# A decoder trunk in fp32: the short convolution's transposes and the attention's value products issued differently

## Chip, cores and metric

One NeuronCore of a Trainium2 chip runs the whole program as one launch. The metric is device time in microseconds (us) of one execution, first to last instruction and what lies around them; the number given is the median of several executions.

## What is computed

Two layers over a sequence of 256 tokens with 1024 features: a half feed-forward block, a mixer, a second half feed-forward block and a gated embedding. The mixer is what the change touches. It projects its normed input to many pieces and runs three branches on them:

```
u = c_gate * xc
y = conv3(u)                       # causal, depthwise, 3 taps along the sequence
y_a = (b_gate * y) @ conv_w_out    # short convolution
y_m = mLSTM(...) @ mlstm_w_out
s = q·k (8 heads, 64 wide, one key and value head), masked to the 64 best keys
y_c = (softmax(s) @ v) @ attn_w_out
merged = g0*y_a + g1*y_m + g2*y_c  # then merged @ w_o
```

## The kernel before

All matrix products are made from fp32 numbers split in two: ScalarE writes the rounded half `wh` of a weight piece (`split`, L157), VectorE the rest `wl` (L158), and TensorE does three products per piece (`mm3`, L205 to L207). Weights come through five `raw` buffers: SyncE issues a transfer (L167) when VectorE has finished with the piece five before it. `project` goes through a projection in ticks of 12 products (4 pieces x 3), and after each tick calls `tick()`, which advances one generator in each of two queues. Those generators hold the side work of the mixer: `queues[0]` the sparse attention `dsa`, `queues[1]` gates and heads of the mLSTM, then `conv`, `conv_gate`, `mlstm_out`. What a generator emits gets a place among the products by a scheduler; every engine then works through its own list in that fixed order, so an instruction that waits holds up all behind it.

Tokens lie on partitions in two blocks `b` of 128; a transpose is needed wherever features must lie on partitions. There are two ways. `turn` (L279) does it on VectorE with 16 transposes of 32x32 pieces, L283. `pe_turn` (L289) does it on TensorE: four 128x128 transposes (L294) into a PSUM tile `tp`, then one copy by ScalarE (L295). There are two `tp` tiles and six PSUM tiles `acc`.

The parts that the change touches, all inside `mixer`:

- `conv` (L731): turns `ccn` to `uT` by `turn`, then 12 instructions of VectorE (L737, L740) make the three taps in `cv`.
- `conv_gate` (L751): turns `cbn` by `turn`, multiplies into `cv` (L755), splits the result (L157, L158).
- the end of `dsa` (L562 to L584): for a query block `b`, the softmax weights `ms` (maximum L551, L552; exponential L554 on ScalarE; L556 and L558 normalise, four heads at a time) are transposed, four heads of one parity `i` and one key block `sb` at a time (L570), copied by ScalarE to `pt` (L572), and multiplied with the values (`value`, L477). The heads of parity 0 write partitions 0 to 63 of their PSUM tile, those of parity 1 partitions 64 to 127. Query block 0 has one key block, query block 1 two. `todo` delays each product by one tick.

Of the kernel before, what the change touches and what calls it, by code (L numbers as in the profile page):

```python
# [13 lines left out]
ALU = mybir.AluOpType  # L14
AX = mybir.AxisListType

P = 128
T = 256
# [19 lines left out]
def trunk_kernel(  # L38
# [23 lines left out]
    def acc():  # L62
        return psum.tile([P, 512], F32, name=nm("acc"), tag="acc", bufs=6)
# [14 lines left out]
    def mid(shape, dt=F32):  # L78
        return spool.tile(list(shape), dt, name=nm("mid"), tag="mid", bufs=7)
# [199 lines left out]
    def turn(dst, src):  # L279

        for i in range(4):
            for j in range(4):
                nc.vector.transpose(  # L283
                    dst[32 * j:32 * j + 32].rearrange("p f (b i t) -> p b f i t", b=NB, i=4)[:, :, :, i, :],
                    src[32 * i:32 * i + 32].rearrange("p b (f j a) -> p b f j a", j=4, a=32)[:, :, :, j, :])
            if i < 3:
                yield
# [151 lines left out]
    def mixer(l, xs, next_norm):  # L439
# [36 lines left out]
        def value(ops, b, i, sb, pt):  # L476
            nc.tensor.matmul(ops[i][i * DH:(i + 1) * DH, :], avn[:, sb, :], pt.rearrange("p j t -> p (j t)"),  # L477
                             start=sb == 0, stop=sb == b)

        def dsa():  # L480
            akT = small([P, 2, T], "akT", 1)
            iqT = half([P, 2, T])
            aqT = mid([P, 4, T])
            for b in range(NB):
                tp = tps()
                for j in range(2):
                    nc.tensor.transpose(tp[:, j, :], kk[:, b, j].rearrange("p a d -> p (a d)"), ident)
                    nc.tensor.transpose(tp[:, 2 + j, :], iqn[:, b, j * P:(j + 1) * P], ident)
                nc.scalar.activation(akT[:, :, blk(b)], tp[:, 0:2, :], AF.Copy)
                nc.scalar.activation(iqT[:, :, blk(b)], tp[:, 2:4, :], AF.Copy)  # L490
                yield
            yield from turn(aqT, aqn)
            yield


            scores = []
            for b in range(NB):
                S = (b + 1) * P
                sc = small([P, S], f"score{b}", 1)
                for j in range(2):  # L500
                    ip = acc()
                    for h2 in range(2):
                        nc.tensor.matmul(ip[:, h2 * S:(h2 + 1) * S], iqT[j * DH:(j + 1) * DH, h2, blk(b)],
                                         akT[j * DH:(j + 1) * DH, 1, 0:S], start=True, stop=True)
                    rl = half([P, 2, S])
                    nc.scalar.activation(rl, ip[:, :2 * S].rearrange("p (a s) -> p a s", a=2), AF.Relu)
                    for h2 in range(2):
                        w = iw[:, b, 2 * h2 + j:2 * h2 + j + 1]
                        if h2 == 0 and j == 0:
                            nc.vector.tensor_scalar(sc, rl[:, h2, :], w, 0.0, op0=ALU.mult, op1=ALU.add)  # L510
                        else:
                            nc.vector.scalar_tensor_tensor(sc, rl[:, h2, :], w, sc, op0=ALU.mult, op1=ALU.add)
                dg = sc[:, b * P:(b + 1) * P]
                nc.gpsimd.affine_select(out=dg, in_=dg, pattern=[[-1, P]], compare_op=ALU.is_ge,
                                        fill=NEG, base=0, channel_multiplier=1)
                scores.append(sc)
                yield
            for b in range(NB):
                sc = scores[b]
                for i in range(N_SEL // 8):  # L520
                    m8 = small([P, 8], "m8")
                    nc.vector.max(out=m8, in_=sc)
                    nc.vector.match_replace(out=sc, in_to_replace=m8, in_values=sc, imm_value=GONE)
                    if i % 2 == 1:
                        yield
                nc.vector.tensor_scalar(sc, sc, -2e38, NEG, op0=ALU.is_ge, op1=ALU.mult)
                dg = sc[:, b * P:(b + 1) * P]
                nc.gpsimd.affine_select(out=dg, in_=dg, pattern=[[-1, P]], compare_op=ALU.is_ge,
                                        fill=NEG, base=0, channel_multiplier=1)
                yield  # L530


            for b in range(NB):
                S = (b + 1) * P
                bias = scores[b]
                ms = big([P, HA, S])
                for g in range(2):
                    for i in range(2):
                        sp = acc()
                        for q in range(2):  # L540
                            nc.tensor.matmul(sp[:, q * S:(q + 1) * S], aqT[i * DH:(i + 1) * DH, 2 * g + q, blk(b)],
                                             akT[i * DH:(i + 1) * DH, 0, 0:S], start=True, stop=True)
                        nc.vector.scalar_tensor_tensor(  # L543
                            ms[:, 4 * g + i:4 * g + 4:2, :], sp[:, :2 * S].rearrange("p (a s) -> p a s", a=2),
                            DH ** -0.5, bias[:, None, :].to_broadcast([P, 2, S]), op0=ALU.mult, op1=ALU.add)
                    yield
                mx = small([P, HA], "mx", 1)
                sm = small([P, HA], "sm", 1)
                for g in range(2):
                    hs = slice(4 * g, 4 * g + 4)  # L550
                    nc.vector.tensor_reduce(mx[:, hs], ms[:, hs, :], axis=AX.X, op=ALU.max)  # L551
                    nc.vector.tensor_scalar(mx[:, hs], mx[:, hs], -1.0, None, op0=ALU.mult)  # L552
                    for h in range(4 * g, 4 * g + 4):
                        nc.scalar.activation(ms[:, h, :], ms[:, h, :], AF.Exp, bias=mx[:, h:h + 1],  # L554
                                             accum_out=sm[:, h:h + 1])
                    nc.vector.reciprocal(sm[:, hs], sm[:, hs])  # L556
                    for h in range(4 * g, 4 * g + 4):
                        nc.vector.tensor_scalar(ms[:, h, :], ms[:, h, :], sm[:, h:h + 1], None, op0=ALU.mult)  # L558
                    yield
                yield  # L560

                ops = []  # L562
                todo = deque()
                for i in range(2):
                    op = acc()
                    ops.append(op)
                    for sb in range(b + 1):
                        tp = tps()
                        for j in range(4):
                            nc.tensor.transpose(tp[:, j, :], ms[:, 2 * j + i, blk(sb)], ident)  # L570
                        pt = half([P, 4, P])
                        nc.scalar.activation(pt, tp, AF.Copy)  # L572
                        todo.append((i, sb, pt))
                        yield
                        if len(todo) > 1:
                            value(ops, b, *todo.popleft())
                while todo:
                    value(ops, b, *todo.popleft())
                yield
                for i in range(2):  # L580
                    rows = slice(i * DH, (i + 1) * DH)
                    split(haT[rows, 0, :, blk(b)], haT[rows, 1, :, blk(b)],
                          ops[i][rows, :].rearrange("p (j t) -> p j t", j=4))
                yield  # L584
# [145 lines left out]

        def conv():  # L731
            uT = mid([P, 4, T])
            yield from turn(uT, ccn)
            yield
            for j in range(4):
                g = [gains[:, G_CONV + 12 * l + 4 * i + j:G_CONV + 12 * l + 4 * i + j + 1] for i in range(3)]
                nc.vector.tensor_scalar(cv[:, j, :], uT[:, j, :], g[2], None, op0=ALU.mult)  # L737
                for i in (1, 0):
                    s = 2 - i
                    nc.vector.scalar_tensor_tensor(cv[:, j, s:], uT[:, j, :T - s], g[i], cv[:, j, s:],  # L740
                                                   op0=ALU.mult, op1=ALU.add)
                yield
# [6 lines left out]
        ybT = big([P, 2, 4, T], F32R)  # L749

        def conv_gate():  # L751
            cbT = mid([P, 4, T])
            yield from turn(cbT, cbn)
            yield
            nc.vector.tensor_tensor(cv, cbT, cv, op=ALU.mult)  # L755
            split(ybT[:, 0], ybT[:, 1], cv)
            yield

# [237 lines left out]
```

## Time and profile before

| | |
|---|---|
| median of 3 runs | 1374.6 us (1374.56 to 1374.91) |
| the profiled execution | 1374.13 us, its span 1372.3 us |
| TensorE busy in the span | 1357.8 us (99%), 6156 products and transposes |
| VectorE busy | 1095.6 us (80%) |
| ScalarE busy | 722.6 us (53%) |
| mean granted TensorE clock | 0.998 of full speed |

Products overlap in TensorE, so its busy time is not the time that they need; the distance from one start to the next is. In the rows below, PE is TensorE, DVE VectorE, ACT ScalarE, SP SyncE; `L570` is line 570; `acc<-wh,xh` means that `acc` is written from `wh` and `xh`; `x4` counts merged instructions.

### The profile page before, as it was taken

To read this page: it belongs to the slowest core of one execution; us is meant where nothing else is said; L and a number is where in the kernel's file an instruction comes from. 1 tells how busy PE (TensorE), PEld (TensorE's weight loads), DVE (VectorE), ACT (ScalarE), POOL (GpSimd) and SP (SyncE) were. 2 spreads that over 40 slices of the span, in tenths; PEclk is the share of its full clock that TensorE was granted. 3 is DMA by queue.
4 is the path that set the end of the run, shared out by engine and by line. 5 is a ranking of instruction groups with operands and counts; after the bars stand their busy time and mean duration, and the time that the engine had idled before them with its cause. 6 is when DMAs were issued, how large, how long until landed. Compare 5 with 4: busy or idle time off the path is not lost.

```text
span 1372.3 us, 17274 instructions
## 1 busy us (share of the span) xinstructions
PE 1357.8 (99%) x6156; PEld 1110.4 (81%) x6156; DVE 1095.6 (80%) x2035; ACT 722.6 (53%) x1135; POOL 24.9 (2%) x42
## 2 busy tenths in 40 slices
PE   9999999999999999999999999999999999999997
PEld 7888888876788888888888888888768888888886
DVE  7988879879965687888788888797799566988876
ACT  6544466565544554444664444666565445444454
POOL 0000000000000000000000000000000000000000
PEclk9999999999999999999999999999999999999999
DMA  7855556533565556655556666565336645556661
GB/s 246 259 187 184 184 181 209 177 124 117 169 230 184 173 181 206 199 194 196 180 153 198 194 205 198 181 184 169 123 123 208 220 157 182 184 187 199 198 208 45
DMA packets 163427, 250.33 MB, mean 182 GB/s; under 512 B 7965, under 2 KB 101261, under 8 KB 163341
## 3 DMA queue, kind: packets, MB, share of 16 engines
q1 hardware_dynamic: 162700, 247.91, 56.6%
q0 software_dynamic: 352, 1.06, 0.2%
q8 instruction: 48, 0.79, 0.2%
q14 instruction: 39, 0.31, 0.1%
q10 hardware_dynamic: 288, 0.26, 0.1%
HBM read 248.14 MB, written 1.06 MB: 182 GB/s over the span
## 4 chain that ended last, share of the span: by engine, by line
PE 93%; DVE 5%; ACT 1%; issue 1%; POOL 0%; POOLq 0%; ACTq 0%
PE acc L205 24%; PE acc L207 24%; PE acc L206 24%; PE acc L402 18%; PE tp L264 2%; DVE mid L283 2%; DVE wl L158 1%; PE acc L693 1%; PE acc L477 1%; DVE mid L740 0%; DVE big L543 0%; DVE mx L551 0%; PE acc L128 0%; PE tp L570 0%; DVE big L558 0%
## 5 line engine op out<-in xcount | busy, mean ns | idle before, releaser
L158 DVE TENSOR_TENSOR wl<-raw,wh 128x1024 fp32r<-128x1024 f32 (+1 forms) x472 | 554.6, 1209 | 102.3 <-ACT wh L157 100.5
L157 ACT ACTIVATE wh<-raw 128x1024 fp32r<-128x1024 f32 (+1 forms) x472 | 473.7, 1043 | 201.3 <-issue 95.0
L205 PE MATMUL acc<-wh,xh 128*128 128x512 f32 (+1 forms) x1384 | 544.8, 394 | 0.8 <-ACT wh L157 0.8
L206 PE MATMUL acc<-wl,xh 128*128 128x512 f32 (+1 forms) x1384 | 538.3, 389 | 0.7 <-DVE wl L158 0.7
L207 PE MATMUL acc<-wh,xl 128*128 128x512 f32 (+1 forms) x1384 | 538.5, 389 | 0.0
L205 PEld LDWEIGHTS acc<-wh,xh 128*128 128x128 f32 x1384 | 260.6, 188 | 57.3 <-issue 3.9
L207 PEld LDWEIGHTS acc<-wh,xl 128*128 128x128 f32 x1384 | 260.3, 188 | 53.0
L206 PEld LDWEIGHTS acc<-wl,xh 128*128 128x128 f32 x1384 | 260.5, 188 | 52.0 <-DVE wl L158 1.2
L283 DVE STREAM_TRANSPOSE half<-half 32x128 f32<-32x128 f32 x640 | 193.9, 303 | 9.5
L402 PE MATMUL acc<-wh,mid 128*128 128x512 f32 x704 | 198.5, 392 | 0.0
L402 PEld LDWEIGHTS acc<-wh,mid 128*128 128x128 f32 x704 | 131.0, 188 | 27.3 <-ACT mid L267 0.9
L402 PE MATMUL acc<-wl,mid 128*128 128x512 f32 x352 | 108.6, 390 | 0.0
L157 ACT ACTIVATE mid<-half 128x512 fp32r<-128x512 f32 x40 | 25.3, 634 | 145.8 <-DVE half L283 145.8
L349 DVE SCALAR_TENSOR_TENSOR half<-acc,r,half 128x256 f32<-128x256 f32 x88 | 42.0, 480 | 74.6 <-ACT half L348 74.6
L348 ACT ACTIVATE half<-acc,r 128x256 f32<-128x256 f32 x88 | 41.5, 473 | 108.4 <-PE acc L207 108.4
L402 PEld LDWEIGHTS acc<-wl,mid 128*128 128x128 f32 x352 | 66.1, 188 | 13.8
L274 ACT ACTIVATE xh<-tp,gains 128x128 fp32r<-128x128 f32 x128 | 41.7, 363 | 19.8 <-PE tp L264 11.4
L206 PE MATMUL acc<-wl,big 128*128 128x512 f32 x128 | 50.0, 391 | 0.0
L207 PE MATMUL acc<-wh,big 128*128 128x512 f32 x128 | 49.9, 390 | 0.0
L205 PE MATMUL acc<-wh,big 128*128 128x512 f32 x128 | 49.8, 389 | 0.0
L275 DVE SCALAR_TENSOR_TENSOR xl<-tp,gains,xh 128x128 fp32r<-128x128 f32 x128 | 40.6, 346 | 8.5 <-ACT xh L274 7.7
L283 DVE STREAM_TRANSPOSE mid<-mid 32x256 f32<-32x256 f32 x96 | 41.8, 436 | 1.5
(184 smaller groups left out, 737.6 us busy)
## 6 DMA issues: line engine op xcount, KB each, us to landing
raw<-in_ffn_w_gu_dram SPq DMA_DIRECT2D x172, 512.0 KB, 5.3
raw<-in_w_in_dram SPq DMA_DIRECT2D x128, 512.0 KB, 4.1
raw<-in_ffn_w_down_dram SPq DMA_DIRECT2D x88, 512.0 KB, 4.7
raw<-in_mlstm_w_out_dram SPq DMA_DIRECT2D x16, 512.0 KB, 3.9
raw<-in_w_o_dram SPq DMA_DIRECT2D x16, 512.0 KB, 4.0
raw<-in_ple_w_gate_dram SPq DMA_DIRECT2D x16, 512.0 KB, 4.5
raw<-in_attn_w_out_dram SPq DMA_DIRECT2D x8, 512.0 KB, 3.7
raw<-in_conv_w_out_dram SPq DMA_DIRECT2D x8, 512.0 KB, 4.8
```

Of the source, the lines that this page charges most:

```text
L157: made = nc.scalar.activation(hi, v, AF.Copy).ins
L158: nc.vector.tensor_tensor(lo, v, hi.bitcast(F32), op=ALU.subtract)
L205: nc.tensor.matmul(ps, ah, wh, start=start, stop=False)
L206: nc.tensor.matmul(ps, ah, wl, start=False, stop=False)
L207: nc.tensor.matmul(ps, al, wh, start=False, stop=stop)
L264: turned[0] = nc.tensor.transpose(tp[:, j, :], src_of(k0 + j), ident).ins
L274: his.append(nc.scalar.activation(hi, tp[:, j:j + 1, :], AF.Copy, scale=g).ins)
L275: nc.vector.scalar_tensor_tensor(lo, tp[:, j:j + 1, :], g, hi.bitcast(F32), op0=ALU.mult, op1=ALU.subtract)
L283: nc.vector.transpose(dst[32 * j:32 * j + 32].rearrange("p f (b i t) -> p b f i t", b=NB, i=4)[:, :, :, i, :], src[32 * i:32 * i + 32].rea ...
L348: nc.scalar.activation(s[:, b, :], ps[b][:, :FCH], AF.Silu, scale=r)
L349: nc.vector.scalar_tensor_tensor(s[:, b, :], ps[b][:, FCH:], r, s[:, b, :], op0=ALU.mult, op1=ALU.mult)
L402: nc.tensor.matmul(dn[b][n], a, w[:, n * 512:(n + 1) * 512], start=c == 0 and f == 0 and a is ah and w is wh, stop=c == NFC - 1 and f == 1 ...
```

## The change

Three edits. `conv` turns `ccn` by `pe_turn`. `conv_gate` transposes `cbn` on TensorE too, four transposes per block, and VectorE multiplies straight out of the PSUM tile. In `dsa` both parities of a key block are transposed and copied before the tick, and their two value products stand side by side behind it.

```
-                ops = []
-                todo = deque()
-                for i in range(2):
-                    op = acc()
-                    ops.append(op)
-                    for sb in range(b + 1):
+                ops = [acc() for _ in range(2)]
+                for sb in range(b + 1):
+                    pts = []
+                    for i in range(2):
                         tp = tps()
                         for j in range(4):
                             nc.tensor.transpose(tp[:, j, :], ms[:, 2 * j + i, blk(sb)], ident)
                         pt = half([P, 4, P])
                         nc.scalar.activation(pt, tp, AF.Copy)
-                        todo.append((i, sb, pt))
-                        yield
-                        if len(todo) > 1:
-                            value(ops, b, *todo.popleft())
-                while todo:
-                    value(ops, b, *todo.popleft())
+                        pts.append(pt)
+                    yield
+                    for i in range(2):
+                        value(ops, b, i, sb, pts[i])
                 yield
...
         def conv():
             uT = mid([P, 4, T])
-            yield from turn(uT, ccn)
-            yield
+            yield from pe_turn(uT, ccn)
...
         def conv_gate():
-            cbT = mid([P, 4, T])
-            yield from turn(cbT, cbn)
-            yield
-            nc.vector.tensor_tensor(cv, cbT, cv, op=ALU.mult)
+            for b in range(NB):
+                tp = tps()
+                for f in range(4):
+                    nc.tensor.transpose(tp[:, f, :], cbn[:, b, f * P:(f + 1) * P], ident)
+                nc.vector.tensor_tensor(cv[:, :, blk(b)], tp, cv[:, :, blk(b)], op=ALU.mult)
+                yield
             split(ybT[:, 0], ybT[:, 1], cv)
```

In the changed kernel some lines have other numbers: 569 for 570, 571 for 572, 733 and 736 for 737 and 740, 744 for 748, 751 and 752 for the new gate, 780 for 782, 783 for 785.

The order on each engine moves in the mixer alone, in both layers alike. First TensorE in query block 1, at the value products. Before, with one product (L477) and one group of four transposes (L570) per tick:

```order
L207 MATMUL acc_2900<-wh_2957,xl_1617 128x512
L477 MATMUL acc_2924<-half_2930,avn_1865 64x512
L570 MATMUL tp_2981<-ident,big_2758 128x128 x4
L205 MATMUL acc_2901<-wh_2957,xh_1680 128x512
L206 MATMUL acc_2901<-wl_2958,xh_1680 128x512
L207 MATMUL acc_2901<-wh_2957,xl_1681 128x512
```

Now, behind the first tick after the transposes of key block 0:

```order
L207 MATMUL acc_2918<-wh_2920,xl_1617 128x512
L477 MATMUL acc_2891<-half_2898,avn_1865 64x512
L477 MATMUL acc_2892<-half_2905,avn_1865 64x512
L569 MATMUL tp_2944<-ident,big_2741 128x128 x4
L569 MATMUL tp_2951<-ident,big_2741 128x128 x4
L205 MATMUL acc_2919<-wh_2920,xh_1680 128x512
L206 MATMUL acc_2919<-wl_2921,xh_1680 128x512
L207 MATMUL acc_2919<-wh_2920,xl_1681 128x512
L751 MATMUL tp_2958<-ident,mid_2656 128x128 x4
```

Both parities stand together, and the first transposes of the convolution's gate (L751) follow three products behind the last softmax transposes. The first softmax transposes of query block 1 stand one tick earlier than before (96 products behind those of query block 0, where it was 108), and the dot products before them (L541) too.

Second, VectorE at the second half of the softmax of query block 1 (`big` is `ms`). Before:

```order
L556 RECIPROCAL sm_2825<-sm_2825 128x4
L740 SCALAR_TENSOR_TENSOR mid_2647<-mid_2741,gains,mid_2647 128x254
L558 TENSOR_SCALAR big_2758<-big_2758,sm_2825 128x256 x4
L551 TENSOR_REDUCE mx_2824<-big_2758 128x4
L158 TENSOR_TENSOR wl_2958<-raw_2963,wh_2957 128x1024
L552 TENSOR_SCALAR mx_2824<-mx_2824 128x4
L283 STREAM_TRANSPOSE mid_2988<-mid_2648 32x2x4x32 x7
L556 RECIPROCAL sm_2825<-sm_2825 128x4
L283 STREAM_TRANSPOSE mid_2988<-mid_2648 32x2x4x32
L558 TENSOR_SCALAR big_2758<-big_2758,sm_2825 128x256 x4
```

Now, where the convolution's taps (L733, L736) stand among the same steps:

```order
L558 TENSOR_SCALAR big_2741<-big_2741,sm_2813 128x256 x4
L733 TENSOR_SCALAR mid_2655<-mid_2750,gains 128x256
L551 TENSOR_REDUCE mx_2812<-big_2741 128x4
L736 SCALAR_TENSOR_TENSOR mid_2655<-mid_2750,gains,mid_2655 128x255
L552 TENSOR_SCALAR mx_2812<-mx_2812 128x4
...
L556 RECIPROCAL sm_2813<-sm_2813 128x4
L736 SCALAR_TENSOR_TENSOR mid_2655<-mid_2750,gains,mid_2655 128x254
L558 TENSOR_SCALAR big_2741<-big_2741,sm_2813 128x256 x4
```

The eight transposes (L283) ahead of the last L558 are gone, as are 16 more at the head of `conv`, and two weight pieces (L158) moved from ahead of it to behind it; the taps of the convolution now stand there, seven of them where "..." is.

Third, ScalarE behind that softmax. Before:

```order
L782 ACT_TABLE_LOAD
L782 ACTIVATE half_2892<-acc_2776,r_1652 128x512
L782 ACTIVATE half_2896<-acc_2777,r_1716 128x512
L157 ACTIVATE wh_3080<-raw_3082 128x1024
L157 ACTIVATE wh_3080<-raw_3086 128x1024
L572 ACTIVATE half_2930<-tp_2925 128x512
```

Now:

```order
L157 ACTIVATE wh_3086<-raw_3088 128x1024
L571 ACTIVATE half_2898<-tp_2893 128x512
L571 ACTIVATE half_2905<-tp_2900 128x512
L780 ACT_TABLE_LOAD
L780 ACTIVATE half_2910<-acc_2788,r_1652 128x512
L780 ACTIVATE half_2914<-acc_2789,r_1716 128x512
L157 ACTIVATE wh_3086<-raw_3092 128x1024
L571 ACTIVATE half_2949<-tp_2944 128x512
L571 ACTIVATE half_2956<-tp_2951 128x512
```

The first two copies of softmax weights stand ahead of the table load and the two sigmoids, the next two behind them and behind one weight piece.

## Rows read from the trace of the kernel before

**Rows 1.** The page's first lines: span, and TensorE's busy time (share) and instructions.

```profile
span 1372.3 us, 17274 instructions
PE 1357.8 (99%) x6156; PEld 1110.4 (81%) x6156; DVE 1095.6 (80%) x2035; ACT 722.6 (53%) x1135; POOL 24.9 (2%) x42
```

**Rows 2.** The chain of work that ended last, one piece of a feed-forward block: start us, us, engine, tile, line, count.

```profile
33.11 5.44 PE acc L402 x24
```

**Rows 3.** Who TensorE waited for, in the whole span: us in total, times, longest us.

```profile
PE tp L570 <- DVE big L558: 4.2, 4, 1.9
```

**Rows 4.** TensorE in order of time, layer 0, around the first softmax transposes of query block 1: start us, us, engine, line, operation, tiles, shape, count, and in brackets the idle time before it and its releaser.

```profile
324.20 0.39 PE L207 MATMUL acc<-wh,xl 128*128 128x512 f32 x1
...
326.72 0.33 PE L570 MATMUL tp<-ident,big 128*128 128x128 f32 x1 [1.90 <-DVE big L558]
...
327.64 0.40 PE L206 MATMUL acc<-wl,xh 128*128 128x512 f32 x1
...
328.11 0.40 PE L205 MATMUL acc<-wh,xh 128*128 128x512 f32 x1
...
332.43 0.39 PE L206 MATMUL acc<-wl,xh 128*128 128x512 f32 x1
```

**Rows 5.** The same instructions in layer 1.

```profile
1002.93 0.39 PE L207 MATMUL acc<-wh,xl 128*128 128x512 f32 x1
...
1006.37 0.40 PE L206 MATMUL acc<-wl,xh 128*128 128x512 f32 x1
...
1006.84 0.40 PE L205 MATMUL acc<-wh,xh 128*128 128x512 f32 x1
...
1009.60 0.39 PE L206 MATMUL acc<-wl,xh 128*128 128x512 f32 x1
```

**Rows 6.** Stretches of both layers around these: window and its length, busy us (instructions) of PE, PEld, DVE, ACT, POOL, granted TensorE clock, DMA share and GB/s.

```profile
324.00:332.00 8.00, 5.90 (x22) 4.27 (x21) 7.82 (x18) 5.66 (x11) 0.00 (x0) 0.79 0.40 129
1002.00:1010.00 8.00, 5.90 (x29) 4.54 (x28) 7.84 (x18) 7.18 (x13) 0.00 (x0) 1.00 0.36 118
```

**Rows 7.** TensorE in order of time at the two value products of query block 0, one of each parity (two instructions each).

```profile
301.33 0.39 PE L207 MATMUL acc<-wh,xl 128*128 128x512 f32 x1
301.65 1.08 PE L477 MATMUL acc<-half,avn 128*64 128x512 f32 x4
302.66 0.50 PE L205 MATMUL acc<-wh,xh 128*128 128x512 f32 x1
303.00 0.39 PE L206 MATMUL acc<-wl,xh 128*128 128x512 f32 x1
```

**Rows 8.** The same at two places of query block 1: one value product of parity 0 with four transposes behind it, and the two of parity 1 behind each other.

```profile
339.07 0.39 PE L207 MATMUL acc<-wh,xl 128*128 128x512 f32 x1
339.38 1.07 PE L477 MATMUL acc<-half,avn 128*64 128x512 f32 x2
340.39 0.66 PE L570 MATMUL tp<-ident,big 128*128 128x128 f32 x4
...
341.12 0.40 PE L206 MATMUL acc<-wl,xh 128*128 128x512 f32 x1
...
343.39 0.39 PE L207 MATMUL acc<-wh,xl 128*128 128x512 f32 x1
...
345.91 0.40 PE L206 MATMUL acc<-wl,xh 128*128 128x512 f32 x1
```

**Rows 9.** The same at four transposes alone between products.

```profile
293.63 0.40 PE L207 MATMUL acc<-wh,xl 128*128 128x512 f32 x1
293.86 0.60 PE L570 MATMUL tp<-ident,big 128*128 128x128 f32 x4
...
294.53 0.40 PE L206 MATMUL acc<-wl,xh 128*128 128x512 f32 x1
```

**Rows 10.** The same at the dot products of half the heads of query block 1.

```profile
308.33 1.14 PE L541 MATMUL acc<-akT,mid 64*128 64x256 f32 x8
```

**Rows 11.** VectorE's groups by line and shape in the whole span: line, engine, operation, tiles, shape, count, then busy us, mean ns of one, idle us before them. The first is `turn` in `dsa`, `conv` and `conv_gate`, 16 each in each layer.

```profile
L283 DVE STREAM_TRANSPOSE mid<-mid 32x256 f32<-32x256 f32 x96 | 41.8, 436 | 1.5
L543 DVE SCALAR_TENSOR_TENSOR big<-acc,score 128x512 f32<-128x512 f32 x8 | 5.3, 684 | 0.1
L551 DVE TENSOR_REDUCE mx<-big 128x4 f32<-128x1024 f32 x4 | 4.8, 1212 | 0.0
L558 DVE TENSOR_SCALAR big<-big,sm 128x256 f32<-128x256 f32 x16 | 4.6, 348 | 0.1
L740 DVE SCALAR_TENSOR_TENSOR mid<-mid,gains,mid 128x255 f32<-128x255 f32 x8 | 3.6, 477 | 0.0
```

**Rows 12.** ScalarE's groups, same columns.

```profile
L572 ACT ACTIVATE half<-tp 128x512 f32<-128x512 f32 x12 | 7.0, 585 | 2.4 <-PE tp L570 2.4
L554 ACT ACTIVATE big<-big,mx 128x256 f32<-128x256 f32 x16 | 7.9, 498 | 15.2 <-DVE mx L552 15.2
L748 ACT ACTIVATE mid<-acc,r 128x512 f32<-128x512 f32 x4 | 2.8, 688 | 5.4 <-PE acc L207 5.4
L782 ACT ACT_TABLE_LOAD x2 | 2.6, 1283 | 0.0
L782 ACT ACTIVATE half<-acc,r 128x512 f32<-128x512 f32 x8 | 5.0, 681 | 0.0
```

**Rows 13.** ScalarE in order of time, a weight piece behind the first copy of query block 1.

```profile
331.95 1.06 ACT L157 ACTIVATE wh<-raw 128x1024 fp32r<-128x1024 f32 x1 [2.31 <-issue]
```

## The prediction

> **What bounds the kernel.** I read the page's first lines, then the chain, TensorE's waits, and the two places where it waits. TensorE is busy 99% of the span [rows 1], and its products go at a fixed pace: 24 of them take 5.44 us, 0.227 each [rows 2]. VectorE and ScalarE matter only where TensorE waits for them, and outside the start there is one such place: the softmax transposes L570 wait for L558, 4.2 us in all [rows 3]. So I price the change on TensorE alone, in three parts: its own work, that wait, and its clock.
>
> The wait stands at the first transposes of query block 1, once in each layer. From the product before it to the second product after it 327.64 - 324.20 = 3.44 us pass in layer 0 [rows 4], and 1006.37 - 1002.93 = 3.44 in layer 1 [rows 5]. The same four transposes with no wait take 294.53 - 293.63 = 0.90 [rows 9], so the wait costs 2.54 us per layer. In layer 0 the granted clock then falls to half, 1.2 GHz: over the stretch it is 0.79, in layer 1 it stays at 1.00 [rows 6]. The same instructions take 332.43 - 328.11 = 4.32 us there and 1009.60 - 1006.84 = 2.76 in layer 1 [rows 4, 5]: 1.56 us lost.
>
> **TensorE's own work.** I call the cost of an insert the time from the start of the last ordinary product before it to the start of the second one after it, less two paces (0.454).
> - Four transposes alone: 0.90 - 0.45 = 0.45 [rows 9].
> - One value product and four transposes: 341.12 - 339.07 = 2.05, cost 1.60 [rows 8].
> - Two value products of one parity: 345.91 - 343.39 = 2.52, cost 2.07 [rows 8].
> - Two of different parities: 303.00 - 301.33 = 1.67, cost 1.22 [rows 7].
>
> The last is the change's lever. A single product holds TensorE from 339.38 to 340.39, 1.01 us [rows 8], and a pair of both parities from 301.65 to 302.66, also 1.01 [rows 7]: the second rides free, since the two write different halves of the partitions. Query block 0 had this already, by chance of `todo`; block 1 had not. Four transposes behind another insert cost 1.60 - 1.22 = 0.38. Four behind four have no row: at least 0.38, at most 0.45, I take 0.42.
>
> Per layer then:
> - Block 1 before: two groups of transposes alone (0.90), two single products with transposes (3.20), the two of one parity (2.07): 6.17. Now eight transposes (0.87), a pair with eight (1.60 + 0.42 = 2.02), four for the gate (0.45), a pair with the gate's other four (1.60): 4.94. So -1.23, with the gate's eight new transposes in it.
> - The convolution's first turn, two groups behind L541: 2 x 0.38 = +0.76.
> - Block 0: eight transposes together instead of four and four, 0.87 for 0.90: -0.03.
>
> That is -0.50, over two layers -1.0 us: the 16 transposes added per layer nearly eat what the pairs give. The Trainium skill, TensorE: Matmul & The Clock Gate, Part 4, puts a 128x128 transpose at about 275 ns in a kernel's context; by it the 16 would add 4.4 us per layer instead of the 1.6 of my rows, and the total below would be about 1372.8. One transpose does last about as long here, but they overlap: a whole group of four costs 0.45 [rows 9], so I keep the rows.
>
> **The wait.** On VectorE 64 of the 96 transposes of `turn` go, 32 x 0.436 = 14 us per layer [rows 11]; 24 of these 32 stood ahead of the L558 that TensorE waited for. By itself this gives nothing; it counts only through the wait. But the scheduler also put the transposes of block 1 one tick (2.72 us) earlier, made them need all eight heads at once, and put the convolution's taps among the softmax steps. So I follow the new chain, from the start of the first L541 of block 1, with durations that leave out most overlap [rows 10 to 12]: L541 1.14, L543 0.68, L551 1.21, four L554 and one L748 on ScalarE 2.68, L543 0.68, four L558 1.15 (busy time over 4); then a tap 0.48, L551 1.21, a tap 0.48, seven taps 3.34 (longer than the four L554 beside them, 1.99), a tap 0.48, four L558 1.15. That is 14.7, and with 0.2 for each of the four tiny L552 and L556 (an estimate, well under the 0.48 of a tap) 15.5 us. TensorE needs, from the same start to the new transposes, 60 products (13.6), L541 twice (2.3) and the two convolution groups (0.76): 16.7. The softmax is ready 1 us early at least, so I take the wait as gone: -2.54 x 2 = -5.1. What is late next has cover: the weight pieces put off behind L558 are made right after it, and their products come a tick and more later.
>
> **The clock.** The fall followed the wait in layer 0, but the same wait in layer 1 had none. I take it as gone with the wait (-1.6); the other end is that it stays (0).
>
> **New waits.** The gate's first transposes need a free `tp`, so the third copy L571. From the end of the tick before the softmax transposes ScalarE does a weight piece 1.06 [rows 13], two copies 1.17, the table load 1.28, two sigmoids 1.36, a weight piece 1.06, the copy 0.59 [rows 12]: 6.5 us. TensorE gets there after 0.87 + 2.72 + 2.02 + 0.68 = 6.3. Even; full durations overstate ScalarE's side. Bounds 0 and, if that weight piece waits 2.31 us for its data as one does in the old trace [rows 13], 2.3; I take the nearer end, 0.1 per layer, +0.2. A `tp` of the gate is freed by VectorE instead of ScalarE, but no transpose needs it until the merge. The weight transfers follow VectorE's pieces, and those before this stage are done earlier; no cost.
>
> **Sum**: -1.0 - 5.1 - 1.6 + 0.2 = -7.5, on 1374.13 of the profiled execution 1366.6. The median of the runs stands 0.5 above that execution, so on its scale **1367.1 us**. A measurement can tell 0.2%, 2.75 us, from no change.
>
> **Rivals.**
> - *ScalarE late at the gate's transposes.* As bounded above: 2.3 - 0.1 = 2.2 us in each layer, 1371.5; if the clock falls after one such wait, 1373.1. For: that weight piece, the sigmoids and the table load all stand ahead of a copy that TensorE waits for. Against: the buffer of that piece's transfer comes free right behind L558, before TensorE comes to the transposes. 0.14, half of it within 0.2%.
> - *The clock falls all the same.* Between the softmax transposes and the last pair some 11 us now hold 24 transposes. If the clock falls there once per layer as it did [rows 4], 1.56 x 2 comes on top: 1370.2. The Trainium skill says in the same Part 4 that transposes do not count as activity for the clock gate. The layer 1 stretch, with a wait and eight transposes at 1.00 [rows 6], speaks against. 0.10.
> - *Block 1's pairs do not overlap*, as they accumulate over two key blocks: 2.07 - 1.22 = 0.85 for four pairs, 3.4 us, 1370.5. 0.03. The change would then do half of what it says.
> - *The transposes at the skill's price*: 1372.8, no change. 0.02.
> - *Slower.* The tap ahead of the second L551 waits for the copy of `uT`, which on ScalarE stands behind a projection's copy (L748), four L554 and a weight piece. If that copy is late, maximum, exponential and L558 are late with it, and TensorE waits with all eight heads. The first 1 us is free; to lose the 7.5 and 2.75 more, it must be 1 + 5.1 = 6.1 us late in each layer. At 7 us it is 6 x 2 = 12 us: 1379.1. The longest wait of ScalarE's weight pieces that my rows show is 2.31 [rows 13]. 0.04.
>
> **The chances.** The forecast has 0.67. Faster by over 0.2%: 0.67 + 0.10 + 0.03 + half of 0.14 = 0.87; within: 0.07 + 0.02 = 0.09; slower 0.04. Low end: ScalarE never late (-0.2), and the edges of inserts that now stand together worth up to 0.2 at four places per layer that I did not count (-1.6): 1365.3. High end: the first rival's 1371.5, which leaves out the last two rivals and the first one's worse half. Range 1365.3 to 1371.5.
>
> **What would show it.** Right: no idle before L569, VectorE's last L558 of block 1 ending 1 us or more ahead of them; L477 in block 1 as x4 in 1.08 us; a granted clock of 1.00 in both layers; 32 L283 of `mid<-mid` left. Wrong: idle before L569 by L558 or before L751 by L571; a half clock in either layer; pairs of 1.9 us.

## The result and the profile after

The changed kernel takes 1366.91 us (median of 4 runs, 1366.83 to 1367.05) against 1374.58 for the kernel before, run beside it (1374.19 to 1374.91): a ratio of 0.9939, 95% interval 0.9927 to 0.9951. Forecast were 1367.1 and a range of 1365.3 to 1371.5. The profiled execution took 1367.05 us, 7.08 less than the one of before.

Its first lines and the shares of the chain, to set beside [rows 1]:

```profile
span 1365.2 us, 17290 instructions
PE 1353.7 (99%) x6188; PEld 1110.4 (81%) x6188; DVE 1069.2 (78%) x1973; ACT 726.1 (53%) x1139; POOL 25.0 (2%) x42
...
PE 98%; ACT 1%; issue 0%; DMA 0%; SPq 0%; DVE 0%; POOLq 0%; POOL 0%; ACTq 0%
```

TensorE has 32 instructions more and is busy 4 us less, VectorE 26 us less: of the 96 transposes of `turn` in [rows 11] 32 are left, 13.9 us. Who TensorE waited for now (us in total, times, longest); the line of [rows 3] has no successor, and all that is left stands at the start:

```profile
PE acc L128 <- DVE warm L123: 1.1, 1, 1.1
PE tp L264 <- DMA x<-in_x_dram: 1.0, 1, 1.0
PE acc L205 <- ACT wh L157: 0.8, 1, 0.8
PE acc L206 <- DVE wl L158: 0.8, 1, 0.8
```

TensorE in order of time in layer 0, from the dot products L541 to the last pair, and then the softmax transposes of layer 1; this answers to [rows 4, 5, 8]:

```profile
305.72 0.39 PE L207 MATMUL acc<-wh,xl 128*128 128x512 f32 x1
306.04 1.14 PE L541 MATMUL acc<-akT,mid 64*128 64x256 f32 x8
307.11 0.66 PE L294 MATMUL tp<-ident,mid 128*128 128x128 f32 x4
...
307.84 0.39 PE L206 MATMUL acc<-wl,xh 128*128 128x512 f32 x1
...
322.71 0.39 PE L207 MATMUL acc<-wh,xl 128*128 128x512 f32 x1
322.94 1.03 PE L569 MATMUL tp<-ident,big 128*128 128x128 f32 x8
...
324.05 0.40 PE L206 MATMUL acc<-wl,xh 128*128 128x512 f32 x1
...
326.32 0.39 PE L207 MATMUL acc<-wh,xl 128*128 128x512 f32 x1
326.64 1.08 PE L477 MATMUL acc<-half,avn 128*64 128x512 f32 x4
327.65 1.09 PE L569 MATMUL tp<-ident,big 128*128 128x128 f32 x8
...
328.82 0.39 PE L206 MATMUL acc<-wl,xh 128*128 128x512 f32 x1
329.05 0.40 PE L207 MATMUL acc<-wh,xl 128*128 128x512 f32 x1
329.29 0.66 PE L751 MATMUL tp<-ident,mid 128*128 128x128 f32 x4
...
330.01 0.39 PE L206 MATMUL acc<-wl,xh 128*128 128x512 f32 x1
...
331.63 0.39 PE L207 MATMUL acc<-wh,xl 128*128 128x512 f32 x1
331.95 1.08 PE L477 MATMUL acc<-half,avn 128*64 128x512 f32 x4
332.96 0.66 PE L751 MATMUL tp<-ident,mid 128*128 128x128 f32 x4
...
333.69 0.40 PE L206 MATMUL acc<-wl,xh 128*128 128x512 f32 x1
...
997.11 1.03 PE L569 MATMUL tp<-ident,big 128*128 128x128 f32 x8
```

No line has a bracket: TensorE waits neither at L569 nor at the gate's L751, and in block 1 both pairs last 1.08 us, as block 0's did [rows 7]. VectorE's second half of the softmax of block 1 and ScalarE's copies ahead of the gate, each in order of time in layer 0, and the windows of [rows 6]:

```profile
314.62 0.34 DVE L733 TENSOR_SCALAR mid<-mid,gains 128x256 f32<-128x256 f32 x1
314.89 1.21 DVE L551 TENSOR_REDUCE mx<-big 128x4 f32<-128x1024 f32 x1
...
319.31 1.14 DVE L558 TENSOR_SCALAR big<-big,sm 128x256 f32<-128x256 f32 x4
```

```profile
323.19 1.06 ACT L157 ACTIVATE wh<-raw 128x1024 fp32r<-128x1024 f32 x1 [2.60 <-issue]
...
327.69 1.05 ACT L157 ACTIVATE wh<-raw 128x1024 fp32r<-128x1024 f32 x1
328.64 1.08 ACT L571 ACTIVATE half<-tp 128x512 f32<-128x512 f32 x2
```

```profile
324.00:332.00 8.00, 8.00 (x42) 5.45 (x41) 7.61 (x13) 5.69 (x9) 0.00 (x0) 1.00 0.95 315
1002.00:1010.00 8.00, 8.00 (x43) 5.75 (x43) 7.86 (x16) 5.60 (x8) 0.00 (x0) 1.00 0.70 244
```

The softmax is ready at 320.45, 2.5 us before TensorE comes at 322.94. The first of the two copies ends near 329.2 and TensorE is at L751 at 329.29: even, as worked out. The clock is 1.00 in both layers.

Where the time went is told best by the start of the same ordinary product in two traces. In front of the first mixer the profiled run of after is 0.5 us late. Such differences, up to 2.3 us against the trace of before (e7), arise in the first 30 us of all these traces; the gains of layers below leave them out, the medians do not. The mixer of layer 0 gains 4.62 us, that of layer 1 2.98, and the stretches between the mixers nothing. I call this **the gain of a layer**. 4.62 + 2.98 - 0.5 = 7.1 is the difference of the profiled executions.

### The profile page after: what moved, and what is told of

Its sections match the earlier page's. It is cut to its first block, busy times and chain, and to the rows that moved or that the text cites. A ratio compares the mean times of both kernels' runs of the same rounds, so it can differ in the third digit from the quotient of the medians.

```text
span 1365.2 us, 17290 instructions
## 1 busy us (share of the span) xinstructions
PE 1353.7 (99%) x6188; PEld 1110.4 (81%) x6188; DVE 1069.2 (78%) x1973; ACT 726.1 (53%) x1139; POOL 25.0 (2%) x42
## 4 chain that ended last, share of the span: by engine, by line
PE 98%; ACT 1%; issue 0%; DMA 0%; SPq 0%; DVE 0%; POOLq 0%; POOL 0%; ACTq 0%
PE acc L205 25%; PE acc L207 25%; PE acc L206 25%; PE acc L402 18%; PE tp L264 2%; PE acc L690 1%; PE acc L541 1%; PE acc L477 0%; PE tp L294 0%; PE tp L569 0%; DMA x<-in_x_dram 0%; PE acc L673 0%; PE acc L503 0%; ACT half L303 0%; SPq L923 0%
## 5 line engine op out<-in xcount | busy, mean ns | idle before, releaser
L158 DVE TENSOR_TENSOR wl<-raw,wh 128x1024 fp32r<-128x1024 f32 (+1 forms) x472 | 554.1, 1208 | 112.8 <-ACT wh L157 111.2
L205 PE MATMUL acc<-wh,xh 128*128 128x512 f32 (+1 forms) x1384 | 543.1, 393 | 0.8 <-ACT wh L157 0.8
L206 PE MATMUL acc<-wl,xh 128*128 128x512 f32 (+1 forms) x1384 | 537.2, 388 | 0.8 <-DVE wl L158 0.8
L207 PE MATMUL acc<-wh,xl 128*128 128x512 f32 (+1 forms) x1384 | 537.3, 388 | 0.0
L207 PEld LDWEIGHTS acc<-wh,xl 128*128 128x128 f32 x1384 | 259.9, 188 | 53.1
L205 PEld LDWEIGHTS acc<-wh,xh 128*128 128x128 f32 x1384 | 259.9, 188 | 52.7 <-ACT wh L157 1.2
L206 PEld LDWEIGHTS acc<-wl,xh 128*128 128x128 f32 x1384 | 260.1, 188 | 52.1 <-DVE wl L158 1.2
L283 DVE STREAM_TRANSPOSE half<-half 32x128 f32<-32x128 f32 x640 | 193.8, 303 | 9.5
L402 PEld LDWEIGHTS acc<-wl,mid 128*128 128x128 f32 x352 | 66.1, 188 | 13.9
L206 PE MATMUL acc<-wl,big 128*128 128x512 f32 x128 | 50.0, 391 | 0.0
L205 PE MATMUL acc<-wh,big 128*128 128x512 f32 x128 | 49.8, 389 | 0.0
L207 PE MATMUL acc<-wh,big 128*128 128x512 f32 x128 | 49.8, 389 | 0.0
L308 POOL TENSOR_TENSOR r<-ms,mhalf 128x1 f32<-128x1 f32 x16 | 10.3, 646 | 1112.1 <-DVE ms L306 550.5
```

The source lines that it names most:

```text
L158: nc.vector.tensor_tensor(lo, v, hi.bitcast(F32), op=ALU.subtract)
L205: nc.tensor.matmul(ps, ah, wh, start=start, stop=False)
L206: nc.tensor.matmul(ps, ah, wl, start=False, stop=False)
L207: nc.tensor.matmul(ps, al, wh, start=False, stop=stop)
L283: nc.vector.transpose(dst[32 * j:32 * j + 32].rearrange("p f (b i t) -> p b f i t", b=NB, i=4)[:, :, :, i, :], src[32 * i:32 * i + 32].rea ...
L402: nc.tensor.matmul(dn[b][n], a, w[:, n * 512:(n + 1) * 512], start=c == 0 and f == 0 and a is ah and w is wh, stop=c == NFC - 1 and f == 1 ...
```

## The experiments

The theory is the prediction's: TensorE's own inserts, one wait for VectorE's softmax and the clock behind it add up to the whole. Rivals: VectorE's relief as such is what pays, or the pairs alone do. Each kernel's ratio is to the kernel before on its own chip. There the medians of the kernel before go from 1374.58 to 1376.0 us, so what sets two of the experiments apart by a microsecond or two is read from the gains of their layers, one trace each, and not from their medians.

### The parts alone

The edits, each against the changed kernel. e1 takes both turns back to VectorE, e3 that of the gate, e4 that of `conv`; e2 takes `dsa` back.

```
 e1 pairs alone, e4 pairs and gate:
-            yield from pe_turn(uT, ccn)
+            yield from turn(uT, ccn)
+            yield
 e1 pairs alone, e3 pairs and conv:
-                for f in range(4):
-                    nc.tensor.transpose(tp[:, f, :], cbn[:, b, f * P:(f + 1) * P], ident)
+            yield from turn(cbT, cbn)
 e2 turns alone:
-                ops = [acc() for _ in range(2)]
+                ops = []
+                todo = deque()
```

> Only the value products are paired; both turns of the convolution stay on VectorE. Additive theory (TensorE's own inserts plus the wait before the softmax transposes plus the clock): per layer the inserts cost 0.87 + 2.02 + 1.22 = 4.11 in block 1 instead of 6.17, and -0.03 in block 0, so -2.1; VectorE still has 16 transposes ahead of the softmax, and its last L558 comes about 1.4 us after TensorE is there, instead of 2.5: -1.1. Together -3.2 per layer, -6.4; with the clock fall of layer 0 gone -8.0: 1366.6 to 1368.2. Rival A (the gain came from VectorE's 14 us per layer): no VectorE work leaves, so 1374.6 or worse, since all eight heads are now wanted one tick earlier. Rival B (the pairs carry all): 1366.9 as the whole change.

> Only the two turns move to TensorE; the value products stand as before. Additive theory: four groups of transposes per layer cost 0.45 + 0.38 + 0.42 + 0.42 = +1.67; the wait of 2.54 goes or shrinks to a few tenths: -0.9 per layer, -1.7 in all, and -1.6 if the clock does not fall: 1371.3 (1371 to 1373). Rival A (VectorE's relief): the whole gain, 1366.9. Rival B (pairs): no gain, 1374.6 to 1378, the transposes being pure cost.

> Pairs, and the convolution's first turn on TensorE; the gate's turn stays on VectorE, where it now stands behind the last L558. Additive theory: like the whole change with the gate's two groups of transposes off TensorE, -0.85 per layer: 1365.2, no wait before the softmax transposes; VectorE's weight pieces two to four ticks later then come just in time, and if they are late it is by under 1 us per layer, up to 1367. Rival A: VectorE carries 7 us per layer more than in the whole change, so between the two kernels, about 1370.

> Pairs, and the gate's turn on TensorE; the convolution's first turn stays on VectorE ahead of the softmax. Additive theory: inserts -2.1 + 0.9 = -1.2 per layer, the wait about 1.4 as with the pairs alone: -1.1; -4.6 in all, -6.2 with the clock fall gone: 1368.4 to 1370.0, so slower than with the pairs alone though VectorE has 7 us less per layer. Rival A: faster than with the pairs alone, about 1370 against 1374.

| | median us | ratio (95%) | wait at the softmax transposes, per layer | gain of layer 0, layer 1 |
|---|---|---|---|---|
| whole change | 1366.91 | 0.9939 (0.9927 to 0.9951) | none | 4.62, 2.98 |
| e1 pairs alone | 1367.42 | 0.9947 (0.9935 to 0.9960) | 1.25 + 0.20 | 4.41, 2.82 |
| e2 turns alone | 1371.62 | 0.9974 (0.9964 to 0.9984) | none | 2.43, 0.86 |
| e3 pairs, conv | 1370.19 | 0.9964 (0.9950 to 0.9978) | none | 3.0, 1.43 |
| e4 pairs, gate | 1369.66 | 0.9959 (0.9947 to 0.9972) | 1.25 + 0.20 | 3.4, 1.87 |

In none of the four does the clock fall in a mixer; layer 0 gains 1.5 to 1.6 more than layer 1 in each, the fall that only the trace of before has there.

e1, e2 and e4 came within their expectations. The rival of VectorE's relief falls from both sides: e1 keeps all of VectorE's transposes and has nearly the whole gain, e2 relieves VectorE by as much as the whole change and has less than half. The pairs as sole cause come closer, but e1 still waits. TensorE in order of time in e1, layer 0:

```profile
321.83 0.39 PE L207 MATMUL acc<-wh,xl 128*128 128x512 f32 x1
322.06 0.38 PE L568 MATMUL tp<-ident,big 128*128 128x128 f32 x2
323.69 0.33 PE L568 MATMUL tp<-ident,big 128*128 128x128 f32 x1 [1.25 <-DVE big L558]
324.22 0.77 PE L568 MATMUL tp<-ident,big 128*128 128x128 f32 x5 [0.20 <-DVE big L558]
...
325.06 0.40 PE L206 MATMUL acc<-wl,xh 128*128 128x512 f32 x1
```

From L207 to the second product after them these eight transposes take 3.23 us, where the whole change takes 324.05 - 322.71 = 1.34: the wait costs 1.89 us a layer. The turns on TensorE that buy it off cost 0.78 + 0.51 + 0.39 = 1.68 (two convolution groups, the gate's four alone, and 1.61 - 1.22 for its four behind a pair [rows 7]; worked out below). The difference of 0.21 is what the whole change is ahead of e1, 0.21 and 0.16 in its layers; the two medians, 0.5 us apart, could not tell them apart. Nearly all of the gain is the pairs': they shorten TensorE's own work, and in their order the eight VectorE transposes that stood ahead of the last L558 stand behind it.

e3 missed its expectation by 5 us. The wait at the transposes is gone as I said, but TensorE waits for weight pieces. Of the seven waits in this line one, of 0.75 us, stands at the start as in every trace; the other six are three in each mixer:

```profile
PE acc L206 <- DVE wl L158: 3.4, 7, 0.8
```

Around one of these waits, VectorE and TensorE in order of time in e3:

```profile
362.79 3.60 DVE L283 STREAM_TRANSPOSE mid<-big 32x256 f32<-32x256 f32 x8
366.42 1.23 DVE L158 TENSOR_TENSOR wl<-raw,wh 128x1024 fp32r<-128x1024 f32 x1
```

```profile
367.70 0.50 PE L206 MATMUL acc<-wl,big 128*128 128x512 f32 x1 [0.29 <-DVE wl L158]
```

With the gate's 16 transposes right behind the last L558, VectorE is busy without a break from there on, and the transposes of `mlstm_out` come to stand ahead of pieces that TensorE wants at once. With the gate's turn off TensorE its layers should have gained 0.85 more than the whole change's; they gained 1.6 less. That these transposes are the cause is read from the order and the waits; no run took them away alone.

### VectorE's chain, longer and shorter

e7 puts eight multiplications ahead of the last normalisation of the changed kernel. e11 is e1 with one instruction put later: `den` times `ssq`, which waits for a power on GpSimd.

```
 e7, in dsa behind the reciprocal:
+                    if b == 1 and g == 1:
+                        for _ in range(8):
+                            nc.vector.tensor_scalar(ms[:, 7, :], ms[:, 7, :], 1.0, None, op0=ALU.mult)
 e11 (and e13), at the end of mlstm_heads and behind drain(heads):
-            nc.vector.tensor_tensor(den, den, ssq, op=ALU.mult)
...
+            if i == 0:
+                nc.vector.tensor_tensor(den, den, ssq, op=ALU.mult)
```

> The whole change with eight more multiplications by 1.0 on VectorE ahead of the last normalisation of query block 1; the scheduler puts three taps and two weight pieces ahead of it too, so that it ends at about 325.8 instead of 320.45 us. TensorE's order is the same. Theory (the change won because VectorE is 2.5 us early there, and nothing else of VectorE counts): TensorE wants the second group's weights at 323.5, so a wait of about 2.3 us a layer comes back: 1366.9 + 4.6 = 1371.5 us, range 1370.5 to 1372.5, plus 1.6 for each layer whose clock falls after that wait as it did once in the trace of before. Rival (the gain came from less VectorE work at large, the wait was a symptom): the eight instructions of 0.27 us are 2.2 of 85 us that VectorE was relieved of in all or less, 1367 to 1368.

> The version with the pairs alone, with one VectorE instruction put later: the last product of den and ssq (L711), which waits 1.57 us for a power on GpSimd while the softmax behind it could start. TensorE's order is the same word for word. Theory (VectorE's chain before the last L558 sets the wait, and it starts late by that instruction): L543 starts at about 309.1 instead of 310.84, the last L558 ends about 1.75 us earlier, and the wait at the softmax transposes (1.25 + 0.2 us a layer) goes: 1367.4 - 2.9 = 1364.5 us, range 1364 to 1365.5, under the whole change's 1366.9. Rival (the wait is held by TensorE's second L541 or by ScalarE's exponentials): 1366.5 to 1367.5, wait still there.

e7: 1370.03 us, ratio 0.9955 (0.9938 to 0.9972); against the whole change each layer loses 1.5 us, and the clock falls in neither mixer. The wait is back, smaller than I expected. VectorE's last normalisation ends at 326.92; this trace is 1.8 us later than that of the whole change in front of the mixer, so that is 325.1 where I had 325.8, and only the last of the eight transposes meets it:

```profile
324.73 0.93 PE L572 MATMUL tp<-ident,big 128*128 128x128 f32 x7
326.97 0.33 PE L572 MATMUL tp<-ident,big 128*128 128x128 f32 x1 [1.31 <-DVE big L561]
```

The median is half a microsecond under my range and 2 above the rival's: the mechanism holds, its size was 2.3 expected and 1.5 measured. The ratio alone would not show it, as its interval overlaps the whole change's; the trace does. The 85 us in the expectation are a slip: by the first lines of the two pages VectorE was relieved of 26.4 us.

e11: 1364.41 us, ratio 0.9917 (0.9903 to 0.9932), 2.5 us under the whole change; against e1 its layers gain 1.63 and 1.67, against the whole change 1.4 and 1.5. VectorE in e1, then in e11:

```profile
310.64 0.17 DVE L711 TENSOR_TENSOR den<-den,ssq 128x8 f32<-128x8 f32 x1 [1.57 <-POOL ssq L710]
310.84 0.69 DVE L543 SCALAR_TENSOR_TENSOR big<-acc,score 128x512 f32<-128x512 f32 x1
...
323.29 1.14 DVE L558 TENSOR_SCALAR big<-big,sm 128x256 f32<-128x256 f32 x4
```

```profile
308.98 0.69 DVE L543 SCALAR_TENSOR_TENSOR big<-acc,score 128x512 f32<-128x512 f32 x1
...
321.50 1.14 DVE L558 TENSOR_SCALAR big<-big,sm 128x256 f32<-128x256 f32 x4
```

The last L558 is 1.79 us earlier, and TensorE has no idle time at the transposes any more. One VectorE instruction of 0.17 us that stood in the wrong place was worth 3 us, where the two turns that the change moved to TensorE bring 0.2 us a layer more than they cost: with it they need not move at all.

### TensorE's transposes, and the clock

e6 issues each of the gate's groups three times, 32 transposes more. e5 is the kernel before again, e13 that kernel with the instruction of e11 put later, e14 that kernel with a longer wait.

```
 e6, in conv_gate:
+                for _ in range(3):
                     for f in range(4):
                         nc.tensor.transpose(tp[:, f, :], cbn[:, b, f * P:(f + 1) * P], ident)
 e14, in dsa behind the reciprocal:
+                    if b == 1 and g == 1:
+                        for _ in range(8):
+                            nc.vector.tensor_scalar(ms[:, 4, :], ms[:, 4, :], 1.0, None, op0=ALU.mult)
```

> The whole change with each group of four gate transposes (L751) issued three times into the same tile: 32 transposes more in all; nothing else changes on TensorE. By the rows (four together 0.109 us each in the stream): +3.5 us, 1370.4, range 1370 to 1371. By the Trainium skill's 275 ns for one (TensorE: Matmul & The Clock Gate, Part 4): +8.8, 1375.7. If transposes do not count as activity for the clock, as the same part says, the granted clock falls to half in the stretch that now holds 40 of them: about 1.6 us a layer more (1373.6 by the rows).

> The kernel of before once more, for its clock: 1374.1 to 1374.9 us. If the fall to half clock after the wait belongs to that place of the kernel, it is in layer 0 again and costs 1.6 us there; if it is chance, it is in the other layer, in both or in none, and the time moves with it by 1.6 for each.

> The kernel of before with one VectorE instruction put later: the product of den and ssq (L715), which waits for a power on GpSimd, goes one instruction back, behind the rest of a split (L158, 0.69 us). TensorE's and ScalarE's order is the same word for word. Theory (the wait of before was VectorE's whole chain, this idle time with it, and the half clock follows only waits of about 1.9 us): VectorE's chain runs 0.69 us earlier, the wait is 1.2 instead of 1.9 us in each layer (-1.4), and no half clock follows, as none followed the waits of 1.25 to 1.31 in three other kernels: -1.6 for each layer that had one, 3.0 to 4.6 us faster than before. Rival (the half clock is chance and has nothing to do with the wait's length): 1.4 us faster, with half clock in one or both layers.

> The kernel of before with eight multiplications of one head's weights by 1.0 ahead of its last normalisation on VectorE; TensorE's order is the same. The wait at the softmax transposes grows from 1.9 to about 4.2 us in each layer. Theory (the half clock follows a wait of TensorE that is long enough): half clock in both layers, 1.6 us each, and 2.1 to 2.3 us more of wait a layer, so 4.2 to 4.6 us slower than before with both falls, 6 slower than a run of before with one. Rival (chance): the clock falls in one layer or none, and the time is 1.6 or 3.2 us less than that.

e6: 1370.72 us, ratio 0.9964 (0.9951 to 0.9977); its layers lose 1.74 and 1.68 against the whole change, 3.42 us for 32 transposes, 0.107 each. The group of twelve, and the clock of the stretch around it:

```profile
331.01 1.53 PE L752 MATMUL tp<-ident,mid 128*128 128x128 f32 x12
...
332.30 0.48 PE L205 MATMUL acc<-wh,xh 128*128 128x512 f32 x1
```

```profile
324.00:338.00 14.00, 14.00 (x81) 10.30 (x80) 13.46 (x24) 9.75 (x13) 0.00 (x0) 1.00 0.69 226
```

e5, one run with a profile: 1377.07 us. It waits 1.9 us in both layers like the trace of before, and the half clock (1.2 GHz) now follows in both: against that trace it loses 1.25 at the start and 1.6 behind the wait of layer 1.

e13: 1371.34 us, ratio 0.9974 (0.9965 to 0.9983). Its waits are 1.07 + 0.20, no half clock follows, and its gains are 2.43 and 0.83. In layer 1, where the trace of before has no fall, that is the shorter wait alone (1.90 - 1.07 = 0.83); in layer 0 the fall's 1.6 come with it.

e14: 1381.23 us, ratio 1.0052 (1.0035 to 1.0069); its profiled execution took 6.8 us more than that of before, where 6 was expected. Its waits are 4.48, half clock follows in both layers, and it loses 2.94 and 3.41. The waits are 4.48 - 2.10 = 2.38 longer; what is left is 0.56 for a longer half clock than in the trace of before in layer 0, and 1.03 for one where that trace has none in layer 1. The windows of e5, and then of e14, in each layer (columns as in [rows 6]):

```profile
324.00:334.00 10.00, 7.88 (x32) 6.05 (x31) 9.75 (x23) 7.60 (x15) 0.00 (x0) 0.83 0.37 110
1004.00:1012.00 8.00, 5.89 (x21) 4.33 (x20) 7.82 (x18) 5.64 (x10) 0.00 (x0) 0.79 0.37 129
```

```profile
328.00:336.00 8.00, 6.32 (x20) 5.09 (x21) 7.84 (x18) 2.78 (x4) 0.00 (x0) 0.57 0.28 82
1010.00:1018.00 8.00, 6.62 (x27) 5.44 (x28) 7.84 (x17) 3.39 (x5) 0.00 (x0) 0.79 0.29 94
```

At these transposes, over all profiles, half clock followed 3 of 4 waits of 1.9 us (before, e5), 2 of 2 of 4.48 (e14), and 0 of 8 of 1.07 to 1.31 (e1, e4, e7, e13). So here the fall goes with the length of the wait, as far as these few counts reach, but not with the layer: which of the waits of 1.9 us is followed by it varies between executions. Why is open, and the length of one wait is not all of it: in the first 30 us TensorE waits 0.8 us at L205 and 0.75 us at L206, 1.5 us apart, in all twelve traces, and in three of them (e3, e6, e7) the clock falls behind these waits and 1.6 us are lost. In e7:

```profile
23.00:27.00 4.00, 3.99 (x11) 3.14 (x12) 3.95 (x8) 2.67 (x3) 0.00 (x0) 0.63 0.76 244
```

By e13's medians the falls are worth 1374.81 - 1371.34 - 2 x 0.83 = 1.8 us to the kernel before, by estimate about one of 1.6 in a run.

## Why the prediction was right, point by point

- **TensorE's own work, -0.50 per layer:** mis-sized by 0.14. By the same rule (start to start, less 0.454) the rows of after give 0.89 for eight transposes alone (324.05 - 322.71), 2.05 for a pair with eight, 0.51 for the gate's four alone, 1.61 for a pair with the gate's other four: 5.06 where I had 4.94. L541 with a convolution group takes 307.84 - 305.72 = 2.12, so a cost of 1.67, and L541 alone, in the trace of before [rows 10], 309.74 - 308.01 = 1.73, so 1.28 by the same rule; the difference is 0.39, and 0.78 for both groups, where I had 0.76. With the -0.03 of block 0 that makes -0.36. The step on the pairs held: both parities in 1.08 us, also over two key blocks.
- **The Trainium skill's price:** TensorE: Matmul & The Clock Gate, Part 4, has about 275 ns for a 128x128 transpose in a kernel's context, in a sentence on bf16; these are f32. The rows agree on how long one lasts (275 in L569's group of after) and not on what one costs: 0.107 us in e6, where at 275 ns the 32 would have cost 8.8 us and cost 3.4.
- **The wait, -2.54 per layer:** gone in both. My chain of at most 15.5 us took 14.4 (320.45 - 306.04), TensorE's way 16.9 where I had 16.7. e7 and e11 show from both sides that this chain decides this wait. Other work of VectorE can bring waits elsewhere, as in e3.
- **The clock, -1.6:** right for the profiled execution: 4.62 - 2.98 = 1.64 between the layers. The other end that I kept (the fall stays) did not come, in a mixer of any kernel with a wait up to 1.31 us or none. That the fall goes with the wait was a guess in the prediction, from one wait with a fall and one without; e5, e13 and e14 bear it out.
- **ScalarE at the gate, +0.1 per layer:** no idle time, within 0.1 us of one. The rival of 2.3 us fell: the weight piece ahead of the gate's copies, at 327.69, follows without idle time. The piece before does wait 2.60, until 323.19, when TensorE has just come to the first transposes; that wait holds up nothing.
- **The rival of the clock by transposes:** fell: after has 24 transposes in those 11 us and e6 has 40, both at a granted clock of 1.00. The Trainium skill's TensorE: Matmul & The Clock Gate, Part 4, says that transposes do not count as busy in the same way as products; in groups of up to twelve between products, as here, no run shows a cost of it.
- **The slower rival** (a tap late ahead of the second L551): not seen. Neither the tap at 314.62 nor the L551 behind it has idle time before it.

The sum: layer 1, free of the clock, should gain 0.50 + 2.54 - 0.1 = 2.94 and gained 2.98; layer 0 should gain 1.56 more, 4.50, and gained 4.62. The terms of TensorE's own work and of ScalarE were off by 0.1 each and to different sides.

That the median came within 0.2 us of 1367.1 is in part luck. The sum was made for the profiled execution: 1366.6, and 1367.05 was measured, with the 0.5 of the late start that no term had. For the median I added the 0.5 by which the runs of before stand above their profiled execution, but those of after stand 0.14 below theirs. The two misses nearly cancel.

What the prediction did not see: part of the wait was not VectorE's work at all. In the trace of before too VectorE stood idle for GpSimd in that chain, and 0.83 us of the wait go with one instruction (e13):

```profile
307.92 0.17 DVE L715 TENSOR_TENSOR den<-den,ssq 128x8 f32<-128x8 f32 x1 [1.27 <-POOL ssq L714]
```

And it priced the two turns as the way to the lost wait, where e1 and e11 show that the pairs and that one instruction get there for less.

## What to carry to other kernels

Price a change on the engine that bounds, in inserts into its stream, and follow the one chain that it waits for from its first instruction; relief of a busy engine counts only there. In that chain look first for idle time inside it: an instruction that waits for a third engine ahead of urgent work is moved for nothing, while moving work to the bounding engine costs on it. Give a piece of work taken off one place of a full engine another look where its scheduler puts it (e3): the weight pieces behind it may be late. That last point is read from order and waits, and no run took it alone.

## What the runs showed of the hardware

- A wait of 1.9 us of TensorE between products is followed by half clock in some executions and not in others, and so are two waits of 0.8 and 0.75 us, 1.5 us apart; the stretch at half clock cost 1.6 us, in e14 1.03 in one layer and 1.56 + 0.56 = 2.1 in the other. Two executions of one program (before and e5) stand 1.6 us apart by the clock alone.
- 128x128 transposes of f32 between products cost TensorE 0.107 us each (e6), where one lasts 0.275 (L569 in after).
- Two value products on different halves of the output partitions take 1.01 us together, as one alone does, also while both accumulate over two key blocks (326.64 to 327.65 in after); two on the same half cost 0.85 more [rows 7, 8].
- A power of 128x8 values on GpSimd holds VectorE, which waits for it, idle for 1.27 to 1.85 us (before, e1, after).
